# A decoder step on one Trainium2 core: two attention steps per gate product instead of three, token-sum rows split at other products and tied to matmuls, weight sums of the up projection tied too

## The chip, the core and the metric

The kernel runs on one core of a Trainium2 chip. The core has five engines, each with its own in-order stream of instructions: TensorE (PE, matrix products, with its weight loads shown apart as PEld), VectorE (DVE), ScalarE (ACT), GpSimd (POOL) and SyncE (SP, which issues DMAs). The engines wait for each other through semaphores. The metric is the device time of one execution in microseconds (us); lower is better. The clock that the throttle grants to TensorE is recorded with every profile, 1.00 being full speed.

## The reference

One layer of a gated decoder step on 1024 prompt tokens and 8x8 sample tokens, all in float32, cut to what matters here:

```python
p = rms_norm(x, ln1) @ w_in                     # D_MODEL = 1024
a, q, k, v, g_a, g_b = split(p)                 # g_a, g_b: 1024 wide each, the gates
A = pooled(a)                                   # causal means over 2/4/8/16 tokens, linear map
attn = combine(dilated_attention(q, k, v))      # 12 heads in 3 groups, window/dilation 128/1, 512/4, 2048/16
mixed = sigmoid(g_a) * (A @ w_pa) + sigmoid(g_b) * (attn @ w_pb)
h = x + mixed @ w_o
y = h + square(relu(rms_norm(h, ln2) @ w_up)) @ w_down     # D_FF = 4096
```

Outputs are y for prompt and sample tokens, the last pooling rows, and updated key/value caches.

## The kernel before, in words

All tokens (1024 prompt and 64 sample, 1088) are held transposed: features over the 128 partitions, tokens along the free axis, in two halves of 544 (H), each processed as two quarters of 272 (Q). Float32 precision is got from two reduced-precision pieces: `split` (L112 to L116) writes a rounded copy with ACT (L114) and the rest, source minus copy, with DVE (L115). `put` (L1253) does the same for a 512-wide weight tile (ACT L1255, DVE L1256). A product of two such pairs takes three passes, hi x hi, hi x lo, lo x hi (`PASSES`), so `products` (L1243) is 2 x 12 = 24 matmuls of 128x272, always written at L1248. The gate projection (8 tiles f of 128 + 128 columns), the up projection and the down projection each compute a 2x2 block product with seven block products instead of eight (Strassen's scheme in Winograd's form). The seven need sums of token rows ("T1" to "T4", "22", kept as split pairs) and sums of weight quarters.

**Order of the work.** Instructions on PE run in the order in which the program is written (`manual_schedule`). For the other engines a scheduler lays out the stream when the kernel is built; it may put an instruction as early as its inputs allow, and each engine then runs its stream strictly in that order. `behind_pe(ins)` (L169) adds a wait: the instruction stays behind the last matmul issued so far in the program (`last_mm`).

**First gate products** (L1453 to L1486). Sixteen units n = 0 to 15, each one `products` call of 24 matmuls, cover block products "11" and "21" for all eight f. `step` (L547) advances generators that run in the background: attention blocks (`attend`, `attention`) and the three-group combination (`combine`: `weights` L727 to L735 on DVE and ACT makes `hl`; PE transposes it, L760 `twg0u`; L769 and L770 weigh the heads). `products` calls `between=step` after each half, and a third `step()` stands at the unit's end (L1476). At the end of the attention, `finish_attention` closes its pools. `put_first(n + 3)` splits the weights of the unit three ahead, tied to unit n.

**Token-sum rows.** `fetch_sums(k)` reads rows for k = 0 to 3 from DRAM (`ts_d`, for k = 3 from the input `xT`) and `split_sums(k)` makes their pairs. Row k = 3 is computed on the spot: four scaled copies (L1319) into `gv0` to `gv3`, four sums and differences (L1321 to L1324) and one more (L1329). The tiles `gv0`, `gv1`, `gv2` have one buffer each, shared by all k, so the work on one k begins when the work on the one before has released them. The splits are done for k = 0, 1, 2, 3 after units 3, 5, 7, 9. `split_t4` does the same for the T4 rows.

**Second gate phase** (`gate_group`, L1385). For each f five units with the prepared rows: T1, T2, T3, 22, T4. `summed` (L1392) makes the weight sum, `put_gate` splits it; `post5` to `post4` add the partial results on DVE, among them L1407, which scales a row read back from DRAM by DMA (`g1_again`). `run` (L1269) prepares each unit two or more ahead of its matmuls.

**Up projection** (L1685 to L1904). First come the "11" and "21" units of the early groups (f < FIRST), their weights put in `apart` and `places` (raw tiles `raw_uf`); meanwhile `make_versions` builds the token rows of the second half: `normed` (L1649), sums and differences over 128x1088 (L1730, `minus`) and their splits (L115). Then T1, T2, T3, 22, T4 per group; `summed` (L1829) makes the weight sums (`sm`, L1831) and `put_up` (L1704) splits them.

Of the kernel before, what the change touches and what calls it, by code (L numbers as in the profile page):

```python
# [10 lines left out]
ALU = mybir.AluOpType  # L11
# [25 lines left out]
def decoder_step(ctx, tc, i, o):  # L37
    nc = tc.nc
    v_, s_, g_, t_ = nc.vector, nc.scalar, nc.gpsimd, nc.tensor
# [44 lines left out]
    act = [[t[:, k, :] for k in range(KD)] for t in act_t]  # L84
# [28 lines left out]
    def split(dst_hi, dst_lo, src):  # L113
        ins = s_.activation(dst_hi, src, AF.Copy)  # L114
        v_.tensor_tensor(dst_lo, src, dst_hi.bitcast(F32), op=ALU.subtract)  # L115
        return ins  # L116
# [430 lines left out]
    def step():  # L547
        for f in [later.pop(0) for _ in range(len(later))]:
            f()
        for r in list(active):  # L550
            if next(r, True):
                active.remove(r)
        cool[0] -= 1
        for r in waiting[:2]:
            if r not in primed:
                primed.add(r)
                next(r)
        if waiting and cool[0] <= 0:
            r = waiting.pop(0)
            if not next(r, True):  # L560
                active.append(r)
            cool[0] = 2
# [645 lines left out]
    def half(j):  # L1208
        return slice(j * H, (j + 1) * H)
# [43 lines left out]
    def put(t, src, marks, shaped=False):  # L1253
        view = (lambda a: a.rearrange("p (k n) -> p k n", n=P)) if shaped else (lambda a: a)
        ins = s_.activation(view(t[:, 0]), src, AF.Copy)  # L1255
        v_.tensor_tensor(view(t[:, 1]), src, view(t[:, 0]).bitcast(F32), op=ALU.subtract)  # L1256
        marks.append(ins)
        return t
# [5 lines left out]
            loads.setdefault(max(0, len(queue) - lead), []).append(load)  # L1264
        queue.append((prep, mm, post))

    got = {}

    def run(ahead=3):  # L1269
        n_prep = len(got)  # L1270
        for n in range(len(queue)):
            for load in loads.get(n, ()):
                load()
            while n_prep < min(len(queue), n + ahead):
                got[n_prep] = queue[n_prep][0]()
                n_prep += 1
            queue[n][1](got.pop(n))
            queue[n][2]()
            if lazy:
                lazy.pop(0)()  # L1280
        queue.clear()
        loads.clear()
# [17 lines left out]
    rows_of = {}  # L1300

    def fetch_sums(k):
        if k == 3:
            rows_of[k] = [gx.tile([P, TOK], F32, name=f"gx{a}") for a in range(2)]
            for a, x in enumerate(rows_of[k]):
                dma(x, i["xT"][:, 4 * a + k, :])
            return
        rows_of[k] = [rr(gx, [P, H], F32, name=f"gv{n}_{k}", tag=f"gv{n}", bufs=1) for n in range(3)]
        for t, slot in zip(rows_of[k], (0, 3, 1)):
            dma(t, ts_d[k][:, slot])  # L1310

    def split_sums(k):

        v = rows_of[k]
        if k == 3:
            v = [rr(gx, [P, H], F32, name=f"gv{n}_{k}", tag=f"gv{n}", bufs=1) for n in (0, 1, 3, 2)]
            for a, x in enumerate(rows_of[k]):
                for j in range(2):
                    v_.scalar_tensor_tensor(two(v[2 * a + j]), by_token(x, j), ln1[:, 4 * a + k:4 * a + k + 1], two(rb_g[j]),  # L1319
                                            op0=ALU.mult, op1=ALU.mult)  # L1320
            v_.tensor_tensor(v[0], v[1], v[0], op=ALU.subtract)  # L1321
            v_.tensor_tensor(v[1], v[3], v[1], op=ALU.subtract)
            v_.tensor_tensor(v[2], v[2], v[3], op=ALU.subtract)
            v_.tensor_tensor(v[2], v[2], v[0], op=ALU.add)  # L1324
            rows_of["t4", k] = v[2]
            v = [v[0], v[3], v[1]]
        for n, row in zip((1, "22", 3), v):
            split(*(t[:, k, :] for t in T[n]), row)
        v_.tensor_tensor(v[0], v[1], v[0], op=ALU.subtract)  # L1329
        split(*(t[:, k, :] for t in T[2]), v[0])  # L1330

# [27 lines left out]
        dma(t, ts_d[k][:, 2])  # L1359

    def split_t4(k):
        split(T[4][0][:, k, :], T[4][1][:, k, :], rows_of.pop(("t4", k)))

    to_prepare = [open_main, lambda: (fetch_t4(0), fetch_t4(1)), lambda: split_t4(0), lambda: (fetch_t4(2), split_t4(1)),
                  lambda: split_t4(2), lambda: split_t4(3)]
# [19 lines left out]
    def gate_group(f):  # L1385
        q = {}

        def get_back():
            back[f] = row_tile(1, f"again{f}")
            behind_pe(dma(back[f], pg_d[f]))  # L1390

        def summed(n, a, b, op):  # L1392
            sums[n] = sum_tile(f"g{n}_{f}")
            behind_pe(v_.tensor_tensor(by_tile(sums[n]), a, b, op=op))
            return put_gate(sums[n])

        def fresh(name):
            q["x"] = xtile(f"pg{f}{name}")
            return [q["x"][:, c] for c in range(2)]

        def more(x):
            return [x[:, c] for c in range(2)]

        def post5():
            q["x5"], q["s5"] = q["x"], gl.tile([P, H], F32, name=f"gt4_{f}", tag="gt4")
            s_.copy(two(q["s5"]), xs_of(q["x"]))
            v_.tensor_tensor(back[f], back[f], rb_g[0], op=ALU.mult)  # L1407

        def post6():
            v_.tensor_tensor(two(back[f]), two(back[f]), xs_of(q["x"]), op=ALU.add)  # L1410

        def post7():
            q["x7"] = q["x"]
            v_.tensor_tensor(two(q["s5"]), two(q["s5"]), xs_of(q["x"]), op=ALU.add)
            v_.tensor_tensor(q["s5"], q["s5"], back[f], op=ALU.add)
            dma_st(g_d[f, 1][:, half(1)], q["s5"])

        def post3():
            z = row_tile(2, f"c{f}")
            v_.tensor_tensor(two(z), two(back[f]), xs_of(q["x5"]), op=ALU.add)  # L1420
            dma_st(g_d[f, 0][:, half(1)], z)

        def post4():
            v_.tensor_tensor(two(back[f]), two(back[f]), xs_of(q["x7"]), op=ALU.add)
            dma_st(g_d[f, 1][:, half(0)], back[f])

        loads.setdefault(max(0, len(queue) - 4), []).append(get_back)
        enqueue(lambda: summed(1, quarter(f, 1, 0), quarter(f, 1, 1), ALU.add),
                lambda A: products(fresh(5), A, B["T1"], True), post5, (lambda: load_gate(f)) if f else None, 7)
        enqueue(lambda: summed(2, by_tile(sums[1]), quarter(f, 0, 0), ALU.subtract),  # L1430
                lambda A: products(fresh(6), A, B["T2"], True), post6)
        enqueue(lambda: summed(3, quarter(f, 0, 0), quarter(f, 1, 0), ALU.subtract),
                lambda A: products(fresh(7), A, B["T3"], True), post7)
        enqueue(lambda: summed(4, quarter(f, 0, 1), by_tile(sums[2]), ALU.subtract),
                lambda A: products(more(q["x5"]), A, B["22"], False), post3)
        enqueue(lambda: put_gate(quarter(f, 1, 1), True),
                lambda A: products(more(q["x7"]), A, B["T4"], False), post4)
# [22 lines left out]
    for n, (f, a) in enumerate(order):  # L1460
        fetch_first(n + 5)
        if a == 0:
            open_x[f] = bank_pair(f"pg{f}")
        products(open_x[f], ready.pop(n), B["21" if a else "11"], a == 0, between=step)
        ready[n + 3] = put_first(n + 3)
        t = row_tile(1 + a, f)
        for c in range(2):
            s_.copy(two(t)[:, c], open_x[f][c][:, :Q])
        dma_st(g_d[f, 0][:, half(0)] if a else pg_d[f], t)
        if n in (3, 5, 7, 9):  # L1470
            split_sums((n - 3) // 2)
        if n in (0, 3, 5):
            fetch_sums(max(0, (n - 1) // 2))
        if n == 2:
            fetch_sums(3)
        step()  # L1476
        if n % 4 == 3 and psx is None and not active and not waiting:
            finish_attention()
        if psx is not None and n > 7:
            prepare_main()  # L1480
        if n == 13:
            for f in range(8):
                gate_group(f)
            for n_prep in range(3):
                got[n_prep] = queue[n_prep][0]()
        if n == 14:  # L1486
            for load in loads.pop(0):
                load()
# [20 lines left out]
    def split_ab(j, k):  # L1509

        t = staged.pop((j, k))
        split(*(abt[j][:, s, k] if k < 4 else act[s][2 + k][:, half(j)] for s in range(2)), t)

    for k in range(6):
        loads.setdefault(8 + 4 * k, []).append(lambda k=k: fetch_ab(0, k))
# [185 lines left out]
    marks_f = []  # L1701
    spot = [0, 0]

    def put_up(src, shaped=False):  # L1704
        spot[0] += 1
        return put(up_spots[spot[0] % 5], src, marks_f, shaped)

    def put_down(w, z):
        spot[1] += 1
# [83 lines left out]
    def group(f, early):  # L1793
# [34 lines left out]

        def summed(n, a, b, op):  # L1829
            sums[n] = sum_tile(f"{n}_{f}")  # L1830
            v_.tensor_tensor(by_tile(sums[n]), a, b, op=op)  # L1831
            return put_up(sums[n])

        def p5():
# [321 lines left out]
```

## Time and profile before

| | |
|---|---|
| time, median of 3 runs | 1439.6 us (1437.29 to 1440.9) |
| the profiled execution's own time | 1438.35 us |
| its span in the trace | 1436.5 us |
| mean granted TensorE clock | 0.995 |
| PE idle behind other engines, the five longest | 5.2, 2.0, 1.39, 1.29, 1.28 us |
| first gate products and attention together | up to 460.49 us |
| second gate phase begins (first T1) | 460.49 us |
| up projection's first unit | 753.01 us |
| up projection's first T1 | 791.54 us |

PE works nearly all the time, in one stream. A row of the timeline or of the list of waits gives start, duration, engine, line, operation, tiles (output <- inputs) and, in brackets, how long the engine stood idle before it and on what. The moment at which a unit of 24 matmuls begins, and the spacing to the next, tell whether PE was held up: undisturbed, the units follow one another every 3.0 us. Start-to-start distance, not duration, is what a DVE or ACT instruction costs its engine, as neighbours overlap a little.

### The profile page before, as it was taken

Reading aid. Unit: us, or ns where it says so; the run is one execution under the profiler, and the core shown is the slowest. Engines: PE = TensorE matmul, PEld = TensorE weight load, DVE = VectorE, ACT = ScalarE, POOL = GpSimd, SP = SyncE. Lnnn points to the kernel's source line nnn. Section 1 sums busy time; section 2 is a strip of 40 time slices with the busy share of each in tenths; the row PEclk is TensorE's granted clock in tenths of the full one; section 3 lists DMA queues with packets and bytes.
Section 4 is the critical chain, followed back from the end, with each engine's and each line's share of the span. In section 5 each row is a group of like instructions: output and inputs, shape, how many; then the busy total and the mean of one; then the engine's idle time right before and its main releaser. Section 6 shows DMA issues by size and latency. Waiting matters only on the chain. (4 is left out here: it accounts for less than half of the span.)

```text
span 1436.5 us, 29403 instructions
## 1 busy us (share of the span) xinstructions
PE 1411.7 (98%) x11101; PEld 1358.2 (95%) x11101; DVE 969.7 (68%) x1795; ACT 751.9 (52%) x1962; POOL 225.6 (16%) x291
## 2 busy tenths in 40 slices
PE   9999999999989999999999999999999999999998
PEld 9988977877879999999999999999999999999998
DVE  7688675756776676786568876666664696665556
ACT  8557755778655223574336544544554544444453
POOL 1711255556500000000001000000000000000100
PEclk9999999999989999999999999999999999999999
DMA  6322898744676676974558667667667987777684
GB/s 211 114 79 108 224 206 219 196 114 100 146 226 219 205 245 205 326 262 150 176 174 253 223 211 254 196 209 243 208 197 252 315 279 266 230 238 223 198 287 166
DMA packets 184204, 300.01 MB, mean 209 GB/s; under 512 B 34423, under 2 KB 91069, under 8 KB 182014
## 3 DMA queue, kind: packets, MB, share of 16 engines
q1 hardware_dynamic: 180990, 254.49, 57.2%
q0 software_dynamic: 3072, 43.65, 9.7%
q8 instruction: 87, 1.43, 0.4%
q14 instruction: 55, 0.45, 0.1%
HBM read 229.66 MB, written 112.06 MB: 238 GB/s over the span
## 5 line engine op out<-in xcount | busy, mean ns | idle before, releaser
L2015 PE MATMUL pd<-places 128*128 128x272 f32 x2688 | 335.0, 287 | 0.3 <-DVE places L1256 0.3
L2015 PEld LDWEIGHTS pd<-places 128*128 128x128 f32 x2688 | 334.6, 188 | 0.6 <-DVE places L1256 0.6
L1255 ACT ACTIVATE places<-raw_d 128x544 fp32r<-128x544 f32 (+1 forms) x176 | 111.1, 646 | 156.2 <-DMA raw_d<-z_d 55.1
L1256 DVE TENSOR_TENSOR places<-raw_d,places 128x544 fp32r<-128x544 f32 (+1 forms) x176 | 122.7, 711 | 92.7 <-ACT places L1255 91.4
L2054 POOL DMA_DIRECT2D out_kv_sample_dram<-in_cache_kv_dram x96 | 47.0, 490 | 837.0 <-ACT places L1255 538.1
L1248 PE MATMUL pz<-act,places 128*128 128x272 f32 x912 | 119.2, 290 | 1.1 <-ACT t L1838 1.1
L1248 PEld LDWEIGHTS pz<-act,places 128*128 128x128 f32 x912 | 116.4, 189 | 1.3 <-ACT t L1838 1.3
L194 PE MATMUL ph<-act,places 128*128 128x272 f32 x768 | 97.0, 289 | 0.0
L194 PEld LDWEIGHTS ph<-act,places 128*128 128x128 f32 x768 | 96.5, 188 | 0.1
L1248 PE MATMUL pz<-act,apart 128*128 128x272 f32 x624 | 82.0, 290 | 0.0
L1248 PEld LDWEIGHTS pz<-act,apart 128*128 128x128 f32 x624 | 79.9, 189 | 0.1
L1248 PE MATMUL pg<-act,places 128*128 128x272 f32 x576 | 79.7, 299 | 0.0
L1248 PEld LDWEIGHTS pg<-act,places 128*128 128x128 f32 x576 | 77.1, 198 | 0.6 <-issue 0.4
L634 POOL TENSOR_TENSOR mr<-ms,mhalf 128x4 f32<-128x4 f32 (+2 forms) x39 | 52.5, 1347 | 105.1 <-DVE ms L633 104.7
L194 PE MATMUL pqk<-places,act 128*128 128x512 f32 x240 | 61.0, 404 | 0.0
L1248 PE MATMUL pz<-places 128*128 128x272 f32 x432 | 56.4, 288 | 0.0
L1248 PEld LDWEIGHTS pz<-places 128*128 128x128 f32 x432 | 55.1, 188 | 0.0
L839 POOL TENSOR_TENSOR pck<-pck,qs 128x256 f32<-128x256 f32 x64 | 47.7, 774 | 42.5 <-DMA pck<-in_cache_kv_dram 12.9
L194 PEld LDWEIGHTS pqk<-places,act 128*128 128x128 f32 x240 | 44.7, 192 | 9.8 <-issue 0.2
L863 POOL TENSOR_TENSOR pcv<-pcv,sc 128x256 f32<-128x256 f32 x64 | 47.1, 765 | 27.5 <-DMA pcv<-in_cache_kv_dram 21.6
L319 PE MATMUL a<-act,places 128*128 128x384 f32 (+1 forms) x288 | 50.3, 333 | 0.9 <-ACT act L297 0.9
L1563 PE MATMUL pab<-ab,places 128*128 128x272 f32 x384 | 50.5, 288 | 0.0
(438 smaller groups left out, 2863.4 us busy)
## 6 DMA issues: line engine op xcount, KB each, us to landing
out_kv_sample_dram<-in_cache_kv_dram POOLq DMA_DIRECT2D x72, 480.0 KB, 5.0
raw_d<-z_d SPq DMA_DIRECT2D x112, 272.0 KB
z_d<-t SPq DMA_DIRECT2D x84, 272.0 KB
raw_d<-in_w_down_dram SPq DMA_DIRECT2D x80, 256.0 KB
raw_u<-in_w_up_dram SPq DMA_DIRECT2D x64, 256.0 KB
raw_qkv<-in_w_in_dram SPq DMA_DIRECT2D x36, 256.0 KB
pck<-in_cache_kv_dram SPq DMA_DIRECT2D x32, 256.0 KB
pcv<-in_cache_kv_dram SPq DMA_DIRECT2D x32, 256.0 KB
```

The source lines that it names most:

```text
L194: last_mm[0] = t_.matmul(out, lhs(a, k), rhs(b, k), start=(j == 0), stop=(j == len(terms) - 1))
L319: last_mm[0] = t_.matmul(pts[m][:, :n], wt[:, a, kk, m * P:(m + 1) * P], act4[b][kk][:, :, part4(c)], start=(p == 0 and kk == 0), stop=(p ...
L634: g_.tensor_tensor(r[:n, :H], ms[:n, :H], mhalf[:n, :H], op=ALU.pow)
L839: behind_pe(g_.tensor_tensor(t[:, n], t[:, n], qs[:, :256], op=ALU.mult))
L863: behind_pe(g_.tensor_tensor(tv, tv, sc[:, j + n, :].unsqueeze(2).to_broadcast([P, 4, HD]), op=ALU.mult))
L1248: last_mm[0] = t_.matmul(x[c][:, :Q], A[:, a, k * P:(k + 1) * P], Bv(b, k, c), start=(first and n == 0), stop=(n == len(terms) - 1), skip_ ...
L1255: ins = s_.activation(view(t[:, 0]), src, AF.Copy)
L1256: v_.tensor_tensor(view(t[:, 1]), src, view(t[:, 0]).bitcast(F32), op=ALU.subtract)
L1563: last_mm[0] = t_.matmul(q[x][:, c, :Q], w.rearrange("p s n -> p (s n)")[:, at:at + P], rhs, start=(n == 0), stop=(n == len(terms) - 1))
L2015: last_mm[0] = t_.matmul(chain[t][:, c, :Q], A[:, a, t * P:(t + 1) * P], Z[:, b, c * Q:(c + 1) * Q], start=(fresh and f == 0 and n == 0), ...
L2054: ins = g_.dma_start(d, a)
```

## The change

Three edits. First, the third `step()` per unit is taken out of the loop of first gate products, so background work advances two steps per unit. Second, the token-sum rows are split after units 3, 6, 9, 11 in the order k = 0, 1, 3, 2 (fetched at 0, 2 for k = 3, 3, 6), their ACT splits are tied to the matmul issued last, as are those of T4 and of the `ab` rows, and L1407 (now L1413) is tied likewise. Third, in the up projection `in_time` ties the weight sums and the ACT part of their splits, from the queue's fourth unit on, to the last matmul issued when the unit is prepared. Lines behind the edits move on by five or six: L1319 becomes L1325, L1321 to L1324 become L1327 to L1330, L1329 becomes L1335, L1394 becomes L1400, L1407 becomes L1413, L1649 becomes L1652, L1730 becomes L1735, L1831 becomes L1836.

```diff
--- before.py
+++ after.py
@@ -1264,7 +1264,12 @@
             loads.setdefault(max(0, len(queue) - lead), []).append(load)
         queue.append((prep, mm, post))
 
-    got = {}
+    got, begun = {}, [0]
+
+    def in_time(ins):
+
+        if begun[0] > 2:
+            behind_pe(ins)
 
     def run(ahead=3):
         n_prep = len(got)
@@ -1272,6 +1277,7 @@
             for load in loads.get(n, ()):
                 load()
             while n_prep < min(len(queue), n + ahead):
+                begun[0] = n_prep
                 got[n_prep] = queue[n_prep][0]()
                 n_prep += 1
             queue[n][1](got.pop(n))
@@ -1325,7 +1331,7 @@
             rows_of["t4", k] = v[2]
             v = [v[0], v[3], v[1]]
         for n, row in zip((1, "22", 3), v):
-            split(*(t[:, k, :] for t in T[n]), row)
+            behind_pe(split(*(t[:, k, :] for t in T[n]), row))
         v_.tensor_tensor(v[0], v[1], v[0], op=ALU.subtract)
         split(*(t[:, k, :] for t in T[2]), v[0])
 
@@ -1359,7 +1365,7 @@
         dma(t, ts_d[k][:, 2])
 
     def split_t4(k):
-        split(T[4][0][:, k, :], T[4][1][:, k, :], rows_of.pop(("t4", k)))
+        behind_pe(split(T[4][0][:, k, :], T[4][1][:, k, :], rows_of.pop(("t4", k))))
 
     to_prepare = [open_main, lambda: (fetch_t4(0), fetch_t4(1)), lambda: split_t4(0), lambda: (fetch_t4(2), split_t4(1)),
                   lambda: split_t4(2), lambda: split_t4(3)]
@@ -1404,7 +1410,7 @@
         def post5():
             q["x5"], q["s5"] = q["x"], gl.tile([P, H], F32, name=f"gt4_{f}", tag="gt4")
             s_.copy(two(q["s5"]), xs_of(q["x"]))
-            v_.tensor_tensor(back[f], back[f], rb_g[0], op=ALU.mult)
+            behind_pe(v_.tensor_tensor(back[f], back[f], rb_g[0], op=ALU.mult))
 
         def post6():
             v_.tensor_tensor(two(back[f]), two(back[f]), xs_of(q["x"]), op=ALU.add)
@@ -1467,13 +1473,10 @@
         for c in range(2):
             s_.copy(two(t)[:, c], open_x[f][c][:, :Q])
         dma_st(g_d[f, 0][:, half(0)] if a else pg_d[f], t)
-        if n in (3, 5, 7, 9):
-            split_sums((n - 3) // 2)
-        if n in (0, 3, 5):
-            fetch_sums(max(0, (n - 1) // 2))
-        if n == 2:
-            fetch_sums(3)
-        step()
+        if n in (3, 6, 9, 11):
+            split_sums({3: 0, 6: 1, 9: 3, 11: 2}[n])
+        if n in (0, 2, 3, 6):
+            fetch_sums({0: 0, 2: 3, 3: 1, 6: 2}[n])
         if n % 4 == 3 and psx is None and not active and not waiting:
             finish_attention()
         if psx is not None and n > 7:
@@ -1509,7 +1512,7 @@
     def split_ab(j, k):
 
         t = staged.pop((j, k))
-        split(*(abt[j][:, s, k] if k < 4 else act[s][2 + k][:, half(j)] for s in range(2)), t)
+        behind_pe(split(*(abt[j][:, s, k] if k < 4 else act[s][2 + k][:, half(j)] for s in range(2)), t))
 
     for k in range(6):
         loads.setdefault(8 + 4 * k, []).append(lambda k=k: fetch_ab(0, k))
@@ -1703,7 +1706,9 @@
 
     def put_up(src, shaped=False):
         spot[0] += 1
-        return put(up_spots[spot[0] % 5], src, marks_f, shaped)
+        t = put(up_spots[spot[0] % 5], src, marks_f, shaped)
+        in_time(marks_f[-1])
+        return t
 
     def put_down(w, z):
         spot[1] += 1
@@ -1828,7 +1833,7 @@
 
         def summed(n, a, b, op):
             sums[n] = sum_tile(f"{n}_{f}")
-            v_.tensor_tensor(by_tile(sums[n]), a, b, op=op)
+            in_time(v_.tensor_tensor(by_tile(sums[n]), a, b, op=op))
             return put_up(sums[n])
 
         def p5():
```

What this does to the streams is shown at three places on DVE. In the names, `cw3` and `hl3` belong to the last combination of heads (u = 3), `raw_gf4_0` is the raw weight tile of unit 8, `twg0u3` the transposed weights on PE.

Before, at the end of the attention:

```order
L732 RECIPROCAL cm3_5593<-cm3_5593 128x8
L733 TENSOR_TENSOR cw3_5595<-ce3_5594,cm3_5593 128x24
L115 TENSOR_TENSOR act1_78<-gv1_2_5754,act0_77 128x544
L735 TENSOR_TENSOR hl3_5596<-cw3_5595,hl3_5596 128x2x12
L761 CAST wT_2052<-twg0u3_5657 24x256
```

With the change:

```order
L732 RECIPROCAL cm3_5656<-cm3_5656 128x8
L733 TENSOR_TENSOR cw3_5658<-ce3_5657,cm3_5656 128x24
L1256 TENSOR_TENSOR places_82<-raw_gf4_0_5555,places_82 128x512
L735 TENSOR_TENSOR hl3_5659<-cw3_5658,hl3_5659 128x2x12
L761 CAST wT_2052<-twg0u3_5719 24x256
```

The split of a token-sum row (k = 2) no longer stands ahead of `hl3`; the split of unit 8's weights does.

The rows of k = 3 before (`gv0_3` is the T1 row, `gapart0` and `gapart1` hold the weight sums of the second gate phase, `rawg0` its raw weights):

```order
L772 TENSOR_TENSOR ocg0b6_5492<-ocg0b6_5492,ow3_2_5608 128x512
L1321 TENSOR_TENSOR gv0_3_5923<-gv1_3_5924,gv0_3_5923 128x544
L1256 TENSOR_TENSOR places_82<-raw_gf5_0_5661,places_82 128x512
L1323 TENSOR_TENSOR gv3_3_5925<-gv3_3_5925,gv2_3_5926 128x544
L115 TENSOR_TENSOR act1_78<-gv2_3_5926,act0_77 128x544
L1322 TENSOR_TENSOR gv1_3_5924<-gv2_3_5926,gv1_3_5924 128x544
L115 TENSOR_TENSOR act1_78<-gv0_3_5923,act0_77 128x544
```

With the change:

```order
L1325 SCALAR_TENSOR_TENSOR gv0_3_5914<-gx0_5551,cols_59,rb_g0_5280 128x544
L1256 TENSOR_TENSOR gapart0_5871<-sm_g1_0_6080,gapart0_5871 128x512
L1256 TENSOR_TENSOR places_82<-sm_g3_0_6088,places_82 128x512
L1256 TENSOR_TENSOR places_82<-rawg0_1_5876,places_82 128x512
L1327 TENSOR_TENSOR gv0_3_5914<-gv1_3_5915,gv0_3_5914 128x544
L1256 TENSOR_TENSOR gapart1_5872<-sm_g2_0_6084,gapart1_5872 128x512
L1328 TENSOR_TENSOR gv1_3_5915<-gv2_3_5917,gv1_3_5915 128x544
L1330 TENSOR_TENSOR gv3_3_5916<-gv3_3_5916,gv0_3_5914 128x544
L115 TENSOR_TENSOR act1_78<-gv0_3_5914,act0_77 128x544
```

The T1 row of k = 3 is now made behind the split weight sums of the second gate phase, where before it stood among the weights of unit 10 (`raw_gf5_0` is unit 9's).

The start of the up projection's T1 before (`sm_1` is the weight sum for T1 of group 0, `apart0` its split; `y1`, `u11` are the token rows of `make_versions`):

```order
L1730 TENSOR_TENSOR u11_9496<-y1_1_8332,u11_9496 128x1088
L115 TENSOR_TENSOR places_82<-u11_9496,places_82 128x1088
L1730 TENSOR_TENSOR y1_0_8331<-y1_0_8331,u11_9496 128x1088
L1831 TENSOR_TENSOR sm_2_0_9825<-sm_1_0_9793,raw_u0_0_9661 128x512
L1256 TENSOR_TENSOR places_82<-sm_3_0_9861,places_82 128x512
L1256 TENSOR_TENSOR apart0_9406<-sm_1_0_9793,apart0_9406 128x512
L115 TENSOR_TENSOR places_82<-u11_9496,places_82 128x1088
L1730 TENSOR_TENSOR y1_0_8331<-y1_0_8331,u11_9496 128x1088
```

With the change:

```order
L1836 TENSOR_TENSOR sm_1_0_9793<-raw_u0_0_9661,raw_u0_1_9662 128x512
L115 TENSOR_TENSOR places_82<-u11_9496,places_82 128x1088
L1735 TENSOR_TENSOR y1_0_8331<-y1_0_8331,u11_9496 128x1088
L1836 TENSOR_TENSOR sm_2_0_9825<-sm_1_0_9793,raw_u0_0_9661 128x512
L115 TENSOR_TENSOR t4_1_9492<-y1_0_8331,t4_0_9491 128x1088
L1836 TENSOR_TENSOR sm_3_0_9861<-raw_u0_0_9661 128x512
L1256 TENSOR_TENSOR apart0_9406<-sm_1_0_9793,apart0_9406 128x512
L115 TENSOR_TENSOR t4_1_9492<-y1_0_8331,t4_0_9491 128x1088
```

The sums `sm_1` to `sm_3` and the split of `sm_1` have moved behind more of the 1088-wide rows: the last split of `u11`, the last difference and the first split for T4 now stand ahead of `apart0`.

## The prediction

> **What bounds the kernel now.** I read the page first, then the list of waits of PE, then PE's timeline from 360 to 530 us and from 750 to 1010 us, the two places which the edits touch.
>
> ```profile
> span 1436.5 us, 29403 instructions
> PE 1411.7 (98%) x11101; PEld 1358.2 (95%) x11101; DVE 969.7 (68%) x1795; ACT 751.9 (52%) x1962; POOL 225.6 (16%) x291
> ```
>
> PE is busy for 98% of the span: 1436.5 - 1411.7 = 24.8 us idle. The change removes no matmul, so it can win or lose only idle time of PE and time at a lower clock. PE's own waits, in total, times and longest:
>
> ```profile
> PE twg0u L760 <- DVE hl L735: 5.2, 1, 5.2
> PE sg0b L671 <- DVE sfm L1054: 1.4, 1, 1.4
> PE pg L1248 <- DVE gt L1414: 1.3, 1, 1.3
> PE pz L1248 <- ACT t L1838: 1.1, 1, 1.1
> ```
>
> These four, 9.0 us in all, are the stalls inside the regions that the edits move, with two of 0.46 and 0.47 us that are quoted below; PE's other waits lie in program stretches with the same instructions in the same places. The largest, in time:
>
> ```profile
> 419.22 0.66 ACT L114 ACTIVATE act<-gv 128x544 fp32r<-128x544 f32 x1 [2.63 <-DMA gv<-ts_d]
> 419.79 0.19 ACT L734 CAST hl<-cw 128x24 fp32r<-128x24 f32 x1
> 419.91 0.73 DVE L115 TENSOR_TENSOR act<-gv,act 128x544 fp32r<-128x544 f32 x1 [1.81 <-ACT act L114]
> 420.56 0.18 DVE L735 TENSOR_TENSOR hl<-cw,hl 128x24 fp32r<-128x24 f32 x1
> 420.88 0.59 PE L760 MATMUL twg0u<-cst,hl 128*24 128x128 f32 x2 [5.23 <-DVE hl L735]
> 421.12 5.59 PE L1248 MATMUL pg<-act,places 128*128 128x272 f32 x24
> 426.55 0.88 PE L769 MATMUL swg0u<-wT,sel 128*128 128x256 f32 x6
> ```
>
> The tiny `hl` sits in ACT's and DVE's streams behind the split of a token-sum row whose DMA is late. The 24 matmuls after it last 426.55 - 421.12 = 5.43 us. The clock in stretches of 3 us (columns: busy time of the engines, then granted clock, DMA share, GB/s) says why:
>
> ```profile
> 400.00:403.00 3.00, 1.80 (x21) 1.68 (x22) 2.71 (x10) 2.00 (x6) 0.00 (x0) 1.00 1.06 382
> 421.00:424.00 3.00, 3.00 (x15) 2.96 (x14) 1.14 (x2) 0.66 (x1) 0.00 (x0) 0.50 0.76 260
> 424.00:427.00 3.00, 3.00 (x17) 3.00 (x17) 1.73 (x3) 1.15 (x3) 0.00 (x0) 0.61 0.34 93
> 427.00:430.00 3.00, 3.00 (x26) 3.00 (x25) 3.00 (x5) 2.19 (x5) 0.00 (x0) 1.00 0.25 93
> ```
>
> The 5.23 us of idleness halved the clock, and it came back only by 427; the 1.39 us wait (it ends at 401.2, within the first of these stretches) left it at 1.00.
>
> **Attention's tail (first edit).** The 1.39 us wait is of the last attention block's scores, whose copy (L657) stood behind `sfm` in DVE's stream; with two steps per unit that copy stands ahead of the weight chain (L727 to L733) and two half products lie before the scores on PE, so it goes. The 5.23 wait goes with the split that made it, and its clock loss with it. What a unit costs at full clock:
>
> ```profile
> 460.49 3.15 PE L1248 MATMUL pg<-act,gapart 128*128 128x272 f32 x24
> 463.48 3.16 PE L1248 MATMUL pg<-places,gapart 128*128 128x272 f32 x24
> ```
>
> 24 matmuls start to start take 463.48 - 460.49 = 2.99 us (0.125 each), so the half clock cost 5.43 - 2.99 = 2.44 us. What comes instead is priced by ACT's rows:
>
> ```profile
> 430.54 0.63 ACT L1255 ACTIVATE places<-raw_gf 128x512 fp32r<-128x512 f32 x1 [1.13 <-PE pg L1248]
> 431.08 0.37 ACT L1468 COPY g<-pg 128x272 f32<-128x272 f32 x1
> 457.71 0.68 ACT L1468 COPY g<-pg 128x272 f32<-128x272 f32 x2 [0.50 <-PE pg L1248]
> ```
>
> The last row's unit ends 2.99 us before T1 starts, at 457.5, so ACT starts 0.25 us after a unit. `hl3` now stands behind the split of unit 8's weights, tied to unit 5's last matmul, and PE's transposition follows unit 5 at once. From that matmul's end: 0.25 us until ACT starts, 0.63 for its part of the split, 0.60 for DVE's part (its price is worked out below), 0.18 for `hl` (its cast on ACT, 0.54 start to start behind the split, a copy and 0.19 long, is done by then) and 0.14 to PE (420.56 + 0.18 to 420.88): 1.8 us, bounds 1.2 and 2.2, too short, by the 1.39 us wait, to lower the clock. Term A: -1.39 - 5.23 - 2.44 + 1.8 = **-7.3** (bounds -7.9 and -6.9).
>
> **The first T1 of the gates (second edit).** Before, k = 3's rows were finished long before T1, which starts at 460.49:
>
> ```profile
> 433.83 1.19 DVE L1319 SCALAR_TENSOR_TENSOR gv<-gx,cols,rb_g 128x544 f32<-128x544 f32 x1
> 435.54 0.71 DVE L1321 TENSOR_TENSOR gv<-gv,gv 128x544 f32<-128x544 f32 x1
> 436.18 0.67 DVE L1256 TENSOR_TENSOR places<-raw_gf,places 128x512 fp32r<-128x512 f32 x1
> 444.34 0.71 DVE L115 TENSOR_TENSOR places<-gv,places 128x544 fp32r<-128x544 f32 x1
> ```
>
> The prices, start to start: a 544-wide row 0.64 (435.54 to 436.18), which is 0.07 under its duration; with the same overlap L1319 1.12 and a 512-wide row 0.60. Now k = 2's rows occupy `gv0` to `gv2` until they are split, and that split is tied to unit 11. So k = 3's three remaining scaled copies, and all that follows, come behind it. PE needs k = 3's rounded T1 row at T1's 4th matmul and its rest at the 8th, that is 4 x 2.99 + 8 x 0.125 = 12.96 us after unit 11's end. DVE's stream from there: ACT takes 0.25 us to start after a unit, 0.65 for two copies (0.68 at 457.71), 0.66 for a split (419.22), so DVE begins at about 1.6 us. Then come, in the order of its stream up to the difference L1327: three scaled copies (3.4), ten 544-wide rows (6.4) and seven 512-wide ones (4.2): 14.0, at 15.6. ACT's rounding of the row follows (0.66), so PE's 4th matmul may start at 16.3. The rest of the row (one weight split, two more differences, the row's own split) takes 2.6 from 15.6: ready at 18.2. PE waits 18.2 - 13.0 = 5.2 in all, 3.9 of it in one piece before the 4th matmul (16.3 against 4 x 2.99 + 4 x 0.125 = 12.4), the rest before the 8th. T2's row follows four 544-wide rows later, 2.6 us, by when PE has 16 matmuls of T1 and 7 of T2 to do (2.9). The stall of 5.23 halved the clock, that of 1.39 did not; one of 3.9 is nearer the longer. If it does, T1 and the next unit run slower, as 32 matmuls in 421 to 427 did against 52 at full clock (20 x 0.125 = 2.5 us lost). I take 1.7 of them. Term B: **+6.9**, bounds +1 (ACT and DVE meet with more overlap than the prices have, and PE comes later) and +8.
>
> [...]
>
> **The stall on L1414 in the second gate phase** goes: it came from a split of `ab` rows and the hoisted L1407, both waiting on a DMA in front of it; L1413 is now tied into its own group. Term C: **-1.3** (0 if another row with a late DMA takes its place).
>
> **The up projection's start (third edit).** DVE is the tight engine here: from 769.54 it is busy without a gap past 800.
>
> ```profile
> 769.54 1.29 DVE L1730 TENSOR_TENSOR u<-y,u 128x1088 f32<-128x1088 f32 x1 [1.72 <-DMA u<-u_d]
> 770.75 1.28 DVE L115 TENSOR_TENSOR act<-y,act 128x1088 fp32r<-128x1088 f32 x1
> 771.95 0.68 DVE L1256 TENSOR_TENSOR apart<-raw_uf,apart 128x512 fp32r<-128x512 f32 x1
> 772.56 1.28 DVE L1730 TENSOR_TENSOR u<-y,u 128x1088 f32<-128x1088 f32 x1
> 776.47 6.19 PE L1248 MATMUL pz<-act,apart 128*128 128x272 f32 x48
> 780.00:800.00 20.00, 19.54 (x156) 19.32 (x155) 20.00 (x24) 13.52 (x20) 0.00 (x0) 1.00 0.87 280
> 791.20 0.68 DVE L1256 TENSOR_TENSOR apart<-sm,apart 128x512 fp32r<-128x512 f32 x1
> 791.54 3.15 PE L1248 MATMUL pz<-act,apart 128*128 128x272 f32 x24
> 796.14 2.29 PE L1248 MATMUL pz<-places,apart 128*128 128x272 f32 x16 [0.46 <-DVE apart L1256]
> ```
>
> A 1088-wide row costs 1.20 (769.54 to 770.75), a 512-wide one 0.60 (771.95 to 772.56). With `summed` tied, the weight sums and splits stand behind more of the wide rows. From 769.54 to the end of `apart0`, the stream now holds 17 wide rows and 9 narrow ones and `apart0` itself: 17 x 1.203 + 9 x 0.602 + 0.68 = 26.55, so 796.1. An early unit's weight split ends, by the same count (6 wide, 1 narrow, itself), at 778.0; its unit starts at 776.47 and wants it at the 9th matmul, 1.0 us on: 0.6 late. The first T1 unit starts at 791.54, so now at 792.1, and wants `apart0` at 793.1: a stall of 796.1 - 793.1, about 2.9. The 0.46 at the next unit goes, as its weights now follow the first ones closely. Half clock would cost some 2 us more; 2.9 lies between 1.39 and 5.23, so I take half, 1.0. Term D: 0.6 + 2.9 - 0.46 + 1.0 = **+4.0**, bounds -0.5 (only the 0.46 goes: the DMA that the stream hangs on comes 3 us earlier) and +6.
>
> **Later in the up projection** the two stalls at 877 to 882 come from sums waiting for raw weights ahead of the adds that free PE's banks:
>
> ```profile
> 872.59 0.69 DVE L1831 TENSOR_TENSOR sm<-raw_u 128x512 f32<-128x512 f32 x1 [5.24 <-DMA raw_u<-in_w_up_dram]
> 873.50 3.17 PE L1248 MATMUL pz<-places 128*128 128x272 f32 x24
> 877.77 3.27 PE L1248 MATMUL pz<-act,places 128*128 128x272 f32 x24 [1.10 <-ACT t L1838]
> 881.51 3.29 PE L1248 MATMUL pz<-t,places 128*128 128x272 f32 x24 [0.47 <-DVE t L1856]
> 884.63 5.57 PE L1248 MATMUL pz<-act,apart 128*128 128x272 f32 x43
> ```
>
> Three units took 884.63 - 873.50 = 11.1 us instead of 3 x 3.0. Tied sums stand after those adds. Behind a tied sum queue the next adds of DVE, and for these waits PE through the banks; each unit leaves 2.99 us for about two narrow splits and sums (1.2) and an add or two (1.3), so the tie costs nothing while that cover of about half a unit holds. Term E: **-2.1**, bounds -2.1 and +3 (64 sums, each 0.08 late).
>
> **Sum**: -7.3 + 6.9 - 1.3 + 4.0 - 2.1 = +0.2. The profiled execution took 1438.35 us (span 1436.5), so 1438.6 is expected of one like it; the median of the runs shown is 1.25 above it, which gives 1439.8. I say 1440, no change.
>
> **Rivals.**
>
> 1. *The two new stalls do not come in this size* (faster). The count of DVE's stream rests on the order and assumes no slack in ACT; if the wide rows start earlier and T1's rows arrive in time, B is +3 and D +1: -7.3 + 3 - 1.3 + 1 - 2.1 = -6.7, 1432.9. For it: the wide rows' start hung on one DMA (the 1.72 us wait at 769.54), and B counts DVE as if nothing of k = 3 could slip forward. Against it: the streams are strict, and k = 2's split cannot come ahead of unit 11. Chance 0.28.
> 2. *The clock gate* (slower): both new stalls lower the clock fully, B +8 and D +6: -7.3 + 8 - 1.3 + 6 - 2.1 = +3.3, 1442.9, and +8.4, 1448.0, if E is at its upper bound too. Middle: 1445. [...] For it: the 5.23 us stall did this. Against: the 1.39 us stall did not. Chance 0.30.
> 3. *Ties late in every group of the up projection* (slower). There are 64 weight sums (16 groups of 4). If each came 0.2 us late, 13 us would be lost: 1453. For it: DVE is full from 780 to 800. Against: half a unit of room later. Chance 0.08.
> 4. *The change does not do what it says*, because the streams keep their order: excluded, since the order shown above moves at all three places. That gains and losses cancel is the forecast: chance 0.34.
>
> **How the numbers follow.** A difference of under 0.3% (4.3 us) can't be told from no change. The forecast's own range is 1436 to 1444. Faster by more: nearly all of rival 1, 0.27. Slower by more: rival 3 and the part of rival 2 above 1443.9, some 0.27 of its 0.30 with the forecast's upper tail: 0.35. The rest, 0.38, is the same. The range reaches from 1431, rival 1's time with T1's stall shorter by another 2 us, to 1449, just past rival 2's upper end, and leaves out rival 3 and the tails.
>
> **What would show it.** In the profile of the changed kernel: no wait of `twg0u` above 2.2 us and the clock at 1.00 around it; T1 of the gates starting near 453.2 with two waits on the k = 3 row of 4 to 6 us in all, one on ACT's `act`, one on DVE's; no wait on L1420; a wait on `apart` of about 3 us at the first T1 of the up projection; none on L1843 or L1861 later. I am wrong if T1's rows are ready before 454 (faster) or if waits on L1256 or L1836 return in group after group (slower).

## The result: no difference that can be measured, and the profile after

| | before | with the change |
|---|---|---|
| time, median of 22 runs each, on the same chip | 1439.64 us | 1440.47 us |
| ratio | | 1.0006, 95% interval 0.9998 to 1.0015 |
| profiled execution: span, mean TensorE clock | 1436.5 us, 0.995 | 1437.2 us, 0.994 |

Four marks on PE's timeline show that the zero is a sum of large parts. First the list of PE's waits with the change (total, times, longest):

```profile
PE pg L1248 <- ACT act L114: 4.1, 1, 4.1
PE pz L1248 <- DVE apart L1256: 2.8, 1, 2.8
PE twg0u L760 <- DVE hl L735: 1.7, 1, 1.7
PE pg L1248 <- DVE act L115: 0.5, 1, 0.5
PE pab L1566 <- DVE act L115: 0.4, 1, 0.4
```

The waits of 5.2, 1.4 and 1.3 us are gone; 4.1, 2.8 and 1.7 have come. In PE's timeline, at the end of the attention, at the gates' first T1 and at the fourth group's T1 (the last row):

```profile
421.14 0.38 PE L760 MATMUL twg0u<-cst,hl 128*24 128x128 f32 x2 [1.68 <-DVE hl L735]
452.21 0.53 PE L1248 MATMUL pg<-act,gapart 128*128 128x272 f32 x3
456.86 1.27 PE L1248 MATMUL pg<-act,gapart 128*128 128x272 f32 x4 [4.11 <-ACT act L114]
458.68 4.22 PE L1248 MATMUL pg<-act,gapart 128*128 128x272 f32 x17 [0.54 <-DVE act L115]
462.70 3.51 PE L1248 MATMUL pg<-places,gapart 128*128 128x272 f32 x24
466.05 3.17 PE L1248 MATMUL pg<-places 128*128 128x272 f32 x24
505.17 3.06 PE L1248 MATMUL pg<-act,gapart 128*128 128x272 f32 x23
```

T1 starts at 452.21 instead of 460.49, 8.3 us earlier. It stops after exactly three matmuls for ACT's rounding of the k = 3 row, and again for DVE's part. T1 and T2 take 466.05 - 452.21 = 13.84 us where before they took 466.48 - 460.49 = 5.99: 7.85 us given back at once. From T3 on to the fourth group's T1 (505.17; 507.19 before) it is 1.6 us shorter: the wait of 1.28 us on L1414 is gone. Before, T3 and the fourth group's T1 were:

```profile
466.48 3.17 PE L1248 MATMUL pg<-places 128*128 128x272 f32 x24
507.19 3.19 PE L1248 MATMUL pg<-act,gapart 128*128 128x272 f32 x24
```

In the up projection, with the change:

```profile
790.53 1.26 PE L1248 MATMUL pz<-act,apart 128*128 128x272 f32 x8
794.63 3.75 PE L1248 MATMUL pz<-act,apart 128*128 128x272 f32 x16 [2.84 <-DVE apart L1256]
798.23 3.18 PE L1248 MATMUL pz<-places,apart 128*128 128x272 f32 x24
801.25 3.17 PE L1248 MATMUL pz<-places 128*128 128x272 f32 x24
876.49 3.17 PE L1248 MATMUL pz<-places 128*128 128x272 f32 x24
885.51 4.68 PE L1248 MATMUL pz<-act,apart 128*128 128x272 f32 x36
```

Its first T1 runs eight matmuls, stands for 2.84 us for the rest of its weights, and the next unit begins 3.71 us later than before (794.52). The first T3 begins at 801.25, 49.7 us after the up projection's first unit (751.53); before, it was 45.3 us (798.27 - 753.01):

```profile
798.27 3.17 PE L1248 MATMUL pz<-places 128*128 128x272 f32 x24
```

The stretch from 873.50 to 884.63 of before is now 876.49 to 885.51, 9.02 us instead of 11.13.

DVE's timeline before T1 is the stream that was counted but for one row: nine 544-wide rows stand in it where ten were counted, with the three scaled copies and the seven 512-wide ones. Its two ends are:

```profile
442.14 1.36 DVE L115 TENSOR_TENSOR act<-gv,act 128x544 fp32r<-128x544 f32 x2 [0.43 <-ACT act L114]
455.41 0.71 DVE L1327 TENSOR_TENSOR gv<-gv,gv 128x544 f32<-128x544 f32 x1
```

From k = 2's split at 442.14 to the difference L1327 that makes k = 3's T1 row, at 455.41, DVE is busy for all of the 13.27 us: the row that PE waits for is made 13.3 us behind the row that held its buffer.

### The profile page after: what moved, and what is told of

The parts are those of the page before. It is cut to its first block, busy times and chain, and to the rows that moved or that the text cites. A ratio compares the mean times of both kernels' runs of the same rounds, so it can differ in the third digit from the quotient of the medians.

```text
span 1437.2 us, 29419 instructions
## 1 busy us (share of the span) xinstructions
PE 1413.6 (98%) x11101; PEld 1359.7 (95%) x11101; DVE 972.5 (68%) x1795; ACT 759.1 (53%) x1962; POOL 227.0 (16%) x291
## 4 chain that ended last, share of the span: by engine, by line
PE 84%; DMA 5%; DVE 5%; ACT 2%; issue 2%; POOL 1%; SPq 1%; DVEq 0%; ACTq 0%; POOLq 0%
PE pz L1248 22%; PE pd L2020 21%; PE pg L1248 10%; PE ph L194 7%; PE pqk L194 5%; PE pv L194 4%; PE a L319 3%; PE pab L1566 2%; PE pq L194 1%; PE pk L194 1%; DMA raw_qkv<-in_w_in_dram 1%; DVE act L115 1%; DVE places L1256 1%; PE pog0b L701 1%; PE sg0b L671 1%
```

## The experiments

All were measured beside the kernel before on the same chip. Ratios are to the kernel before; the change itself stands at 1.0006.

**1. The first edit alone.** Two steps per unit, everything else as before.

```diff
-        step()
         if n % 4 == 3 and psx is None and not active and not waiting:
```

> Only the first edit: two steps per unit, token-sum rows and up projection as before. Theory of the prediction (the first edit alone takes away the 5.23 us wait): twg0u3's wait falls below 2.2 us and the gate's T1 starts some 7 us earlier, 1432 to 1434 us. Rival (the wait went because the second edit tied the token-sum splits; untied, DVE's stream now holds all the splits of k = 1 to 3 ahead of hl3): the wait of PE at twg0u3 grows to 10 to 20 us, half clock behind it, T1 of the gates later than 460.5, time 1446 to 1456 us.

Measured: 1448.35 us, ratio 1.0072 (1.0059 to 1.0085), slower. Its list of PE's waits has:

```profile
PE twg0u L760 <- DVE hl L735: 7.1, 2, 3.8
PE sft L1069 <- DVE sres L1064: 6.7, 1, 6.7
```

PE's timeline:

```profile
423.64 1.09 PE L1069 MATMUL sft<-cst,sres 128*128 128x64 f32 x4 [6.65 <-DVE sres L1064]
437.88 0.59 PE L760 MATMUL twg0u<-cst,hl 128*24 128x128 f32 x2 [3.79 <-DVE hl L735]
471.25 3.15 PE L1248 MATMUL pg<-act,gapart 128*128 128x272 f32 x24
```

DVE's timeline ahead of the transposition:

```profile
435.26 0.73 DVE L115 TENSOR_TENSOR places<-gv,places 128x544 fp32r<-128x544 f32 x1
437.10 0.18 DVE L733 TENSOR_TENSOR cw<-ce,cm 128x24 f32<-128x24 f32 x1
```

A last token-sum row is split at 435.26, between the small steps of the weight chain, whose product `cw` comes only at 437.10: untied splits go ahead of the attention's small work. T1 of the gates starts at 471.25, 10.8 us later than before. The direction of the rival, but not its picture: no single wait of 10 to 20 us, but 3.36, 6.65 and 3.79 at three places of the same chain.

**2. The second edit alone.** Rows split after 3, 6, 9, 11 and tied; three steps; no ties in the up projection.

```diff
+        step()
         if n % 4 == 3 and psx is None and not active and not waiting:
...
-        if begun[0] > 2:
+        if False:
```

(against the changed kernel)

> Only the second edit: three steps per unit as before, rows split after units 3, 6, 9, 11 and tied, up projection as before. If the tie is what freed hl3: no 5.23 us wait although three steps are kept, the 1.39 us wait behind sfm stays, the T1 stall of the gates is there in full (4.1 + 0.5 us, half clock, 7.9 us in all), the wait on L1416 is gone; -5.2 - 2.4 + 7.9 - 1.6 = -1.3, so 1437 to 1440 us. If the first edit freed it: the 5.23 us wait is still there, +7.9 - 1.6 = +6, 1446 us.

Measured: 1439.91 us, ratio 1.0013 (1.0001 to 1.0025). PE's timeline:

```profile
412.58 0.38 PE L760 MATMUL twg0u<-cst,hl 128*24 128x128 f32 x2
449.75 0.54 PE L1248 MATMUL pg<-act,gapart 128*128 128x272 f32 x3
455.25 1.27 PE L1248 MATMUL pg<-act,gapart 128*128 128x272 f32 x4 [4.96 <-ACT act L114]
457.07 4.22 PE L1248 MATMUL pg<-act,gapart 128*128 128x272 f32 x17 [0.55 <-DVE act L115]
```

PE reaches the transposition without any wait, with three steps kept; the wait of 1.4 us behind `sfm` is gone too, which neither theory had. The T1 stall is there in full (4.96 + 0.55). So the tie freed `hl`, and the same edit makes the T1 stall.

**3. The token-sum ties taken out of the changed kernel**, distances and order kept.

```diff
-            behind_pe(split(*(t[:, k, :] for t in T[n]), row))
+            split(*(t[:, k, :] for t in T[n]), row)
```

> The changed kernel with only the ties of the token-sum splits (rows 1, 22 and 3 of T) taken out; distances, order of k, the other ties and two steps stay. Theory (ties, not distances, keep DVE's stream free for hl3): all rows are hoisted ahead of hl3 again, PE waits 10 to 20 us at twg0u3, T1 of the gates has its rows in time (its 4.1 us wait gone), 1446 to 1456 us. Rival (the distances do it): twg0u3's wait stays under 3 us, T1's stall goes, 1433 us.

Measured: 1452.48 us, ratio 1.0098 (1.0077 to 1.012). The waits are those of experiment 1 again, and T1 has its rows in time:

```profile
PE twg0u L760 <- DVE hl L735: 7.6, 2, 4.2
PE sft L1069 <- DVE sres L1064: 6.8, 1, 6.8
PE pz L1248 <- DVE apart L1256: 4.8, 2, 3.9
```

The gates' T1 starts at 470.13 without a wait. It is the tie, not the later unit in the program, that keeps the rows off DVE during the attention; and T1's stall is the price of the tie. (The third line is the start of the up projection, whose ties this kernel keeps.)

**4. The third edit alone**, `in_time` added to the kernel before.

```diff
+    def in_time(ins):
+        if begun[0] > 2:
+            behind_pe(ins)
...
+        in_time(marks_f[-1])
...
-            v_.tensor_tensor(by_tile(sums[n]), a, b, op=op)
+            in_time(v_.tensor_tensor(by_tile(sums[n]), a, b, op=op))
```

> Only the third edit, ties in the up projection. Theory: 4.4 us lost at its first T1 (a wait on apart of 2.8 us and half clock behind it), 2.1 us won around 877 to 882: +2.3, 1442 us. Rival (half of the loss belongs to the earlier arrival of PE in the changed kernel): wait on apart under 2 us, 1440 us or less.

Measured: 1441.62 us, ratio 1.002 (1.001 to 1.003). DVE's timeline:

```profile
773.50 1.29 DVE L1738 TENSOR_TENSOR u<-y,u 128x1088 f32<-128x1088 f32 x1 [2.47 <-DMA u<-u_d]
```

PE's timeline:

```profile
782.06 5.29 PE L1248 MATMUL pz<-act,apart 128*128 128x272 f32 x40 [0.92 <-DVE apart L1256]
800.82 3.78 PE L1248 MATMUL pz<-act,apart 128*128 128x272 f32 x16 [3.22 <-DVE apart L1256]
```

Loss at the first T1 and no stall around 880, as forecast, and 2.5 us slower (1441.62 against 1439.14 of the kernel before on that chip) where 2.3 were expected. An early PE, the rival, is not the reason: T1 begins 22.8 us after DVE's first `u` row (796.32 - 773.50), before it was 22.0 (791.54 - 769.54), so PE comes to that stream later, not earlier. New is the size: 0.92 + 3.22 us of waits against 2.84 in the changed kernel's profile, with a wait of DVE on the DMA of `u_d` of 2.47 us against 0.66 there.

**5. k = 2 ahead of k = 3.**

```diff
-        if n in (3, 6, 9, 11):
-            split_sums({3: 0, 6: 1, 9: 3, 11: 2}[n])
+        if n in (3, 6, 8, 10):
+            split_sums({3: 0, 6: 1, 8: 2, 10: 3}[n])
```

> The changed kernel, but k = 2 is split after unit 8 and k = 3 after unit 10 (it was k = 3 after 9 and k = 2 after 11). Theory (k = 3 waits for the gv buffers that k = 2 holds until unit 11): T1 of the gates waits for nothing, clock stays at 1.00 there, 7.8 us less than the changed kernel: 1432 to 1433 us. Rival (DVE is simply full before T1, any order is late): the stall stays within 2 us of its size, or moves to the weight sums gapart, 1438 us or more.

Measured: 1436.19 us, ratio 0.9974 (0.9964 to 0.9984): 4.6 us under the change by the ratios (1.0006 - 0.9974 = 0.32%), where 7.8 were expected. PE's timeline:

```profile
452.26 1.15 PE L1248 MATMUL pg<-act,gapart 128*128 128x272 f32 x8
454.12 2.29 PE L1248 MATMUL pg<-act,gapart 128*128 128x272 f32 x16 [0.70 <-DVE gapart L1256]
459.24 3.17 PE L1248 MATMUL pg<-places 128*128 128x272 f32 x24
787.33 1.27 PE L1248 MATMUL pz<-act,apart 128*128 128x272 f32 x8 [1.20 <-ACT apart L1255]
791.67 4.00 PE L1248 MATMUL pz<-act,apart 128*128 128x272 f32 x16 [3.08 <-DVE apart L1256]
```

DVE's, in the stream ahead of `apart0`:

```profile
784.32 1.29 DVE L1735 TENSOR_TENSOR y<-y,u 128x1088 f32<-128x1088 f32 x1 [1.76 <-DMA y<-u_d]
```

The mechanism holds: T1 and T2 take 459.24 - 452.26 = 6.98 us instead of 13.84, and what is left is 0.70 on the weight sums. The rest is lost in the up projection, whose first unit to first T3 takes 52.8 us (746.10 to 798.89) against 49.7 in the changed kernel. Its T1 waits 1.20 + 3.08 us here, after 0.92 at an early unit: its DVE stream hangs on a DMA (a wait of 1.61 us for `u_d` in this profile) and starts 4.5 us earlier where PE comes 5.4 us earlier, and it stands for another 1.76 us on its way, for a row that the changed kernel's profile has in time.

**6. Up ties only behind the first groups.**

```diff
-        if begun[0] > 2:
+        if begun[0] > 18:
```

> The changed kernel with the up projection's ties starting only behind the first groups of the queue (from its 20th unit on instead of the 4th). Theory: the stall at the first T1 of the up projection goes (4.4 us with its half clock), the 2.1 us won around 877 to 882 stay won: 1436 us. Rival (the tie's gain and its loss are the same rows): the two stalls at 877 to 882 or others like them come back, 1438 us.

Measured: 1433.54 us, ratio 0.9962 (0.9949 to 0.9975), 6.3 us under the change by the ratios. In PE's timeline the stall at the first T1 is gone, only the 0.66 us at the next unit is back:

```profile
788.32 3.15 PE L1248 MATMUL pz<-act,apart 128*128 128x272 f32 x24
793.13 2.29 PE L1248 MATMUL pz<-places,apart 128*128 128x272 f32 x16 [0.66 <-DVE apart L1256]
```

No wait on the adds stands in its list, so the later ties give all of the gain and the early ones all of the loss. That more than 4.4 us was won fits experiments 4 and 5, in whose profiles the early ties cost more than in the changed kernel's own: from the first unit to the first T3 they have 51.9 and 52.8 us, against 45.3 before.

**7. Both repairs together** (5 and 6).

> Both: k = 2 after unit 8, k = 3 after unit 10, and late up ties. Theory: the two gains add, 7.8 + 4.4 = 12.2 us below the changed kernel: 1428 us, faster than both kernels by more than 0.6%. Rival (time won ahead of the up projection is lost again in waits for DMA): 1431 us or more.

Measured: 1429.93 us, ratio 0.9927 (0.9914 to 0.994). The two add: 0.9974 + 0.9962 - 1.0006 = 0.993. Between the two expectations in microseconds, and 0.7% faster than both kernels.

**8 and 9. What the third step is worth**, with both repairs in: three steps again, and two steps beside it on the same chip. Against experiment 7's kernel, the first has the line back and the second is that kernel:

```diff
+        step()
         if n % 4 == 3 and psx is None and not active and not waiting:
```

> The kernel with both repairs (k = 2 after unit 8, k = 3 after unit 10, late up ties) and three steps per unit again, so without the first edit. Theory (the tie alone freed hl3, two steps only bring a 1.7 us wait at twg0u3): no wait at twg0u3, T1 of the gates starts near 450, 2 to 3 us below the kernel with both repairs and two steps: 1427 us. Rival (two steps are needed to keep the 1.4 us wait behind sfm away, and that outweighs): same as with two steps within 1 us, or slower.

> The kernel with both repairs and two steps a second time, on the chip of the run before it, for the comparison: 1429 to 1430 us, T1 of the gates 2 to 3 us later than there, a wait of 1.7 us at twg0u3.

Measured: three steps 1428.66 us, ratio 0.991 (0.9895 to 0.9925); two steps 1429.07 us, 0.9914 (0.9898 to 0.9931). The wait of 1.68 us at `twg0u` is there with two steps and not with three, but the time can't tell them apart: the first theory's 2 to 3 us did not show. In the profiles T1 starts at 452.73 with three steps and at 457.50 with two, but experiment 7, the same kernel with two steps, has 454.57: most of this is scatter from before the gates. Counted from the first gate product (382.82, 386.62 and 383.63), T1 begins after 69.9 us with three steps and after 70.9 in both profiles with two: 1 us. With three steps PE's timeline has:

```profile
437.52 15.37 PE L1248 MATMUL pg<-act,places 128*128 128x272 f32 x120 [1.49 <-ACT g L1474]
```

and ACT's:

```profile
435.73 0.66 ACT L114 ACTIVATE act<-gv 128x544 fp32r<-128x544 f32 x1 [2.86 <-DMA gv<-ts_d]
```

A split of a k = 2 row waits 2.86 us for its DMA in ACT's stream ahead of the copies (L1474) for which PE's matmuls wait 1.49 us; with two steps the like costs 1.33 us, so this is a cost of splitting k = 2 after unit 8 and not of the steps. That 1 us lies within the scatter of the times (1427.01 to 1430.5 and 1427.78 to 1433.19).

## Why the prediction was right, and where its steps were not

The forecast, +0.2 us on the profiled execution and no change, met +0.7 in span. Term by term, from the marks of the two timelines:

| term | predicted | measured | from |
|---|---|---|---|
| A, attention's tail | -7.3 | -8.3 | T1 starts 452.21 against 460.49 |
| B, T1 of the gates | +6.9 | +7.85 | T1 start to T3 start, 13.84 against 5.99 |
| C, the wait on L1414 | -1.3 | -1.6 | T3 start to the fourth group's T1 |
| D, start of the up projection | +4.0 | +4.5 | its start to the first T3, 49.7 against 45.3 |
| E, its later part | -2.1 | -2.1 | 9.02 against 11.13 |
| not foreseen | | +0.5 | gates to up projection, with 0.4 us on `pab` |

Together 0.9 us, and the spans differ by 0.7. Behind these marks a wait of 0.66 us at 1093, which the prediction's list had left out, is gone as well, and one on the down projection's weights has grown from 0.34 to 1.02 us. The signs and sizes held, because DVE's stream before T1 and before the up projection's T1 could be counted: 13.3 us from k = 2's split to L1327 against 14.0 (one 544-wide row fewer), waits of 4.11 + 0.54 against 5.2, of 2.84 against 2.9, of 1.68 at `twg0u` against 1.8.

That the sum came so close is in part luck: A and C gave 1.3 us more than forecast, B, D and the unforeseen term took 2.0 us more. And each column is one execution: two executions of one kernel (experiments 7 and 9) start T1 2.9 us apart, so the 1.0 us by which A was missed can't be assigned. Which tie of the second edit removes the wait of term C was not tested.

**What failed is the attribution of term A.** The prediction headed it "Attention's tail (first edit)" and let the 5.23 us wait go "with the split that made it". Experiments 1 to 3 show that the split moved because the second edit tied it. Without the tie, two steps per unit cost some 9 us; with the tie, three steps have no wait at all there, and the 1.4 us wait, explained by the half products of the first edit, is gone as well (why, no run shows). So A belongs to the second edit, A and B are gain and price of the same tie, and all that the first edit is seen to bring there is the 1.68 us wait, which in the time of experiments 8 and 9 could not be seen.

**Sizes that were off:** the half clock at T1. Of B's 7.85 us, 4.65 are waits and 3.2 the slower clock (0.50 from 456.6 to 463.5), for which 1.7 of an estimated 2.5 were taken, a choice that no run shows. The waits are 0.6 us under the 5.2 counted, but not because the row was early: the four matmuls between them ran at a clock of 0.50 too, and T1's eighth matmul began 6.5 us after its first (458.68 - 452.21) where the count has 6.2 (18.2 - 4 x 2.99). At the up projection the early unit lost 0.3 us instead of 0.6, and the clock (0.50 from 794.5 to 798.0) 1.6 (16 matmuls in 3.60 us, 794.63 to 798.23, instead of 2.0) instead of 1.0.

**D was right for the changed kernel's profile but is not a constant.** Its count left PE and DVE at their old moments, though A to C bring PE forward. Both came earlier by nearly as much, PE's first unit by 1.5 us (751.53 against 753.01), DVE's first `u` row by 1.8 us (767.72 against 769.54); nothing in the count assured that. The prediction's lower bound rested on an earlier DMA; experiments 3 to 5 show the other direction, with up to 5.2 us of waits at the same place (0.92 + 1.20 + 3.08).

Four profiles with the early ties show where the size comes from: the changed kernel's and those of experiments 4, 3 and 5, in this order. From the first `u` row to the end of `apart0`'s split DVE takes 26.9, 27.3, 28.0 and 28.4 us, and PE's waits at T1 are 2.84, 3.22, 3.92 and 4.28 us, each time 24.0 to 24.1 us less. The count for this stream was 26.55. What comes on top are DVE's waits inside it for later rows from `u_d`: none, 0.58, 1.24 and 1.76 us. The wait ahead of the stream (0.66, 2.47, 1.51 and 1.61 us) does not put them in order. This is read from profiles; no run moved that DMA by itself.

Of the rivals, the first (both stalls shorter) did not come. The second (both at half clock) came in so far as the clock was 0.50 behind both stalls, with B (7.85) near its +8 and D (4.5) nearer the forecast's +4.0; the time stayed at the forecast as A and C had more to give. The third (ties late in every group) is refuted: no unit of the up projection behind the first T1 waits for a tied sum.

## What to carry to other kernels

When a scheduler may hoist work into a stream that also carries short, urgent instructions, a tie to the matmul stream frees these; but the tied work then starts at the tie, so count, in the new order, everything that stands between the tie and the consumer, buffers included, and put the row that is needed first, or whose buffers others need, ahead. Start ties only where the stream has room: here the same tie won 2 us in the steady part of the up projection and lost 4.5 to 7.5 us at its start, where DVE was busy for 28.14 of 28.28 us (767.72 to 796 with the change). And when gains and losses of one change cancel, separate them by run: reordering two rows and delaying one set of ties turned the zero into a gain of 0.7 to 0.9%.

## What the runs showed of the hardware

Behind some of PE's waits the granted clock of TensorE was 0.50 for some microseconds, behind others it stayed at 1.00. The moments can be worked out from stretches of 0.4 us (after the length stand the busy times of PE, PEld, DVE, ACT and POOL with their counts, then granted clock, DMA share and GB/s), first of the kernel before:

```profile
388.40:388.80 0.40, 0.00 (x0) 0.00 (x0) 0.23 (x1) 0.40 (x4) 0.00 (x0) 0.98 0.64 173
388.80:389.20 0.40, 0.00 (x0) 0.00 (x0) 0.07 (x1) 0.40 (x3) 0.00 (x0) 0.50 1.03 302
395.20:395.60 0.40, 0.40 (x4) 0.17 (x5) 0.40 (x1) 0.00 (x0) 0.00 (x0) 0.50 0.57 212
395.60:396.00 0.40, 0.40 (x8) 0.40 (x10) 0.40 (x3) 0.00 (x0) 0.00 (x0) 0.99 0.83 305
419.20:419.60 0.40, 0.00 (x0) 0.00 (x0) 0.00 (x0) 0.38 (x1) 0.00 (x0) 0.88 1.21 258
419.60:420.00 0.40, 0.00 (x0) 0.00 (x0) 0.09 (x1) 0.38 (x2) 0.00 (x0) 0.50 1.32 306
426.00:426.40 0.40, 0.40 (x3) 0.40 (x3) 0.40 (x1) 0.00 (x0) 0.00 (x0) 0.59 0.24 87
426.40:426.80 0.40, 0.40 (x6) 0.40 (x5) 0.36 (x2) 0.01 (x1) 0.00 (x0) 1.00 0.00 0
```

and of the changed kernel:

```profile
456.40:456.80 0.40, 0.00 (x0) 0.00 (x0) 0.40 (x2) 0.40 (x1) 0.00 (x0) 0.78 0.69 269
456.80:457.20 0.40, 0.34 (x1) 0.34 (x2) 0.40 (x1) 0.01 (x1) 0.00 (x0) 0.50 0.34 129
463.20:463.60 0.40, 0.40 (x4) 0.40 (x4) 0.40 (x2) 0.35 (x1) 0.00 (x0) 0.69 0.00 0
463.60:464.00 0.40, 0.40 (x5) 0.40 (x5) 0.40 (x2) 0.00 (x0) 0.00 (x0) 1.00 0.19 60
794.40:794.80 0.40, 0.17 (x1) 0.17 (x1) 0.40 (x2) 0.24 (x1) 0.00 (x0) 0.68 0.99 346
794.80:795.20 0.40, 0.40 (x2) 0.40 (x3) 0.40 (x1) 0.00 (x0) 0.00 (x0) 0.50 1.03 394
797.60:798.00 0.40, 0.40 (x4) 0.40 (x4) 0.00 (x0) 0.00 (x0) 0.00 (x0) 0.55 0.66 112
798.00:798.40 0.40, 0.40 (x5) 0.40 (x5) 0.00 (x0) 0.00 (x0) 0.00 (x0) 1.00 0.61 82
```

Before, the clock was 0.50 from 388.8 to 395.6, where PE had waited 1.29 and 2.05 us on `sg0b` (to 387.09 and to 389.63), and from 419.5 to 426.3, where it had waited 5.23 us (to 420.88): 6.8 us each time. The wait of 1.39 us that ended at 401.20 left it at 1.00. In the changed kernel the clock was 0.50 from 456.6 to 463.5 (6.8 us), where the 4.11 us wait at T1 ended at 456.86, and from 794.5 to 798.0 (3.4 us), where the 2.84 us wait of the up projection ended at 794.63; the wait of 1.68 us at `twg0u` that ended at 421.14 left it at 1.00.

So T1's stall had 6.8 us of half clock behind it, and the stall of the up projection 3.4 us. Within the first, PE stood once more, for 0.54 us, and within the second not at all; whether that made the difference is not shown. Two other profiles have the same lengths: 6.8 us at the gates' T1 in experiment 6 (454.0 to 460.8) and 3.4 us at the up projection's T1 in experiment 4 (800.8 to 804.2). Why one wait is followed by half clock and another is not, no run shows.
